# Products ahead of a norm: the first weight tiles run on the unnormalised residual

## The chip, the cores and the metric

The kernel runs on one core of a Trainium2 chip. The metric is the device time of one execution in microseconds, the median of several runs; the shorter, the better.

## The reference, cut to what matters

The input x is [256 tokens, 1024 features] in float32. The first block adds three mixers, a gated convolutional feed-forward net (FFN) and a gate; then come a pooling layer, an FFN, a dilated attention and another FFN. Each of these reads a root-mean-square norm of the residual, and the ones of the second part are modulated: each feature gets a scale and a shift computed from a condition vector c.

```
def _rmsnorm(x, g):
    x32 = x.astype(jnp.float32)
    y = x32 * lax.rsqrt(jnp.mean(x32 * x32, axis=-1, keepdims=True) + EPS)
    return (y * g.astype(jnp.float32)).astype(x.dtype)

def _modulate(h, shift, scale):
    return h * (1 + scale[:, None, :]) + shift[:, None, :]

h = h + rms_norm(mix, post_mix_norm[i])
f = conv_ffn(rms_norm(h, pre_ffn_norm[i]), w_up[i], conv_w[i], conv_b[i], w_down[i])

def _conv_ffn(h, w_up, conv_w, conv_b, w_down):
    a, v = jnp.split(h @ w_up, 2, axis=-1)
    a = _causal_dwconv(a, conv_w, conv_b)
    return (jax.nn.silu(a) * v) @ w_down
```

The factor of a token (the rsqrt) multiplies a whole row of the norm's output, so a product with a weight matrix may take it before or after.

## The kernel before, in words

Activations lie with features on the 128 partitions: x is `xT`, 8 tiles of 128 features x 256 tokens. Every product is computed to nearly float32 by splitting both sides in a high and a low part: `wr`, `wl` of a weight tile (ScalarE L208 or L211, VectorE L209 or L212) and `R`, `L` of an activation tile. `mm3` (L222 to L224) issues R wr, L wr and R wl; an output tile of 128 features over 1024 inputs is one weight tile and 24 such matmuls of 128x256. Weight tiles come in order from the SP queue; TensorE's sums lie in six buffers `acc`.

A norm goes so: while the last product before it is made, each x tile is squared on ScalarE (`sq`), GpSimd adds the squares up (L251), and TensorE sums them over the partitions (`st <- ones, sq`, L239). `rstd` turns the sums into token factors: VectorE `rv` (L263), GpSimd `rr` (L265), and TensorE spreads them over the partitions (`st <- cst, rr`). `norm_split` then makes, for each of 8 tiles, `ny` = x g rb on VectorE (L288), R on ScalarE (L275 or, with a shift, L278) and L on VectorE (L276, L279); the next products start when the first R and L are there.

Four places matter:
- first norm: `post` (L1077 to L1090) norms the mixer's output F, adds it to x tile by tile (VectorE: F <- F, st at L1088, xT <- xT, F at L1090) and sums the squares of x; then `norm_split` and the products of w_up, the first FFN;
- second: behind `ple_gate`; then pool_w_in and the pooling chain on VectorE (`ps`, L1200 to L1203);
- third: behind pool_w_out (`addg`, L1110); then ffn_w_up0;
- fourth: behind attn_w_o (`addg`); then ffn_w_up1, the last FFN.

The norm ahead of the attention is not touched. The modulation vectors are computed along the way: `ada_rows` (L994 to L1006) loads a weight row group `adw` in four transfers and runs 32 small matmuls on it (`acc <- adw, ccol`), a ScalarE copy `row` and a transpose (`acc <- cst, row`), placed at norms; `ada` does single columns on VectorE (L1051). `ple_vec` norms a side input p (`acc <- pT, raw`).

The order on each engine is set by a scheduler that goes by priority: `norm_split` and `rstd` are marked as high priority, and in `post` the order on VectorE is the program's (`manual_schedule`). `wload` keeps later weight splits behind the last split of a norm (`keep_free`).

Of the kernel before, what the change touches and what calls it, by code (L numbers as in the profile page):

```python
# [9 lines left out]
F32 = mybir.dt.float32  # L10
F32R = mybir.dt.float32r
# [6 lines left out]
T = 256  # L18
D = 1024
KB = 8  # L20
# [6 lines left out]
# modulation columns per weight tile: mixer output, FFN up (every other tile), FFN down, pool, layer 0 up and down,  # L27
# attention, gate
# [15 lines left out]
ORDER = "uswrcSn"  # L44
RATE = ((0,1),(3,2),(2,2),(1,1))

# [27 lines left out]
def _consts():  # L74
    """shape-only constants: masks, identities, distance tables"""
# [15 lines left out]
    d = 128 + p - s                                                   # query 128 + p, key s  # L91
# [40 lines left out]
class Net:  # L132
# [28 lines left out]
    def c(self, name):  # L161
        o, n = COFF[name]
        return self.cst[:, o:o + n]
# [9 lines left out]
    # ------------------------------------------------------------------ setup  # L173
    def setup(self):
# [3 lines left out]
        self.cst = self.const([128, NCST], "cst")  # L178
        nc.sync.dma_start(self.cst[:, 0:128], a["cst"][:, 0:128])
# [5 lines left out]
        self.ident, self.bones, self.cen = self.c("ident"), self.c("bones"), self.c("cen")  # L185
        self.mAR = self.c("mAR").rearrange("p (a t) -> p a t", a=2)
        self.mD, self.mOT, self.blk, self.hsel, self.idc = (self.c(n) for n in ("mD", "mOT", "blk", "hsel", "idc"))
# [6 lines left out]
        self.L = self.const([128, KB, T], "L", F32R)  # L194

    # ------------------------------------------------------- weight streaming
    def wload(self, W, m, k0, kn, width=128):
        """W: DRAM [mt, 128, kb*width]; returns hi and lo parts as [128, kn, width]."""
# [59 lines left out]
    def rstd(self, st, r=None):  # L258
        """token sums of squares [128, 2] -> PSUM [128, T] with rsqrt(mean + eps) on every partition"""
# [11 lines left out]
    def split(self, y, R, L, bias=None):  # L271
        """R + L = y (+ bias), both parts exact in float32r"""
# [18 lines left out]

    def keep_free(self, hold):
# [18 lines left out]
    def mixers(self, rb):  # L311
        tc, a = self.tc, self.a
        with tc.tile_pool(name="mx", bufs=1) as mx, tc.tile_pool(name="mxp", bufs=2, space=PSUM) as self.px:
            self.mx = self.tp = mx
            self.rbs = self.mxt([128, T], "rbs")
# [20 lines left out]
    def mix_rw(self):  # L336
# [7 lines left out]
        # feature tiles of w_in: 0-2 r, 3-5 k, 6-8 v, 9 decay|aaa, 10 gate, 11-13 q, 14 kc, 15 vc,  # L344
        # 16 ks, 17 kw, 18-19 s5
        for m in (9, 10, 3, 4, 5, 0, 1, 2, 6, 7, 8):
            pz = self.psum("acc", self.nacc)
            self.lin(W, m, pz[:, 0:T], self.R, self.L, chunk=4 if m == 9 else KB)
            if m == 10:
                nc.sync.dma_start(self.cst[:, 128:NCST], a["cst"][:, 128:NCST])  # L350
# [73 lines left out]
    def rwkv(self):  # L424
# [32 lines left out]
        # cumulated log decays per chunk of 64 tokens  # L457
# [1035 lines left out]
```

## Time and profile before

| | |
|---|---|
| median of 3 runs | 1277.03 us (1273.57 to 1280.05) |
| profiled execution, first to last instruction (span) | 1274.8 us |
| its mean granted TensorE clock | 0.954 |
| busy: TensorE, VectorE, ScalarE, GpSimd | 94%, 72%, 53%, 9% |

The profile gives no time of the profiled execution beside its span, so the span stands for it. In a row, PE is TensorE (PEld its weight loads), DVE VectorE, ACT ScalarE, POOL GpSimd; `out<-in` are the program's tile names, and a number in brackets is the time for which the engine was idle before, with what ended it. A granted clock of 1.00 is 2.4 GHz and of 0.50 is 1.2 GHz.

### The profile page before, as it was taken

To read this page: it belongs to the slowest core of one execution; us is meant where nothing else is said; L and a number is where in the kernel's file an instruction comes from. 1 tells how busy PE (TensorE), PEld (TensorE's weight loads), DVE (VectorE), ACT (ScalarE), POOL (GpSimd) and SP (SyncE) were. 2 spreads that over 40 slices of the span, in tenths; PEclk is the share of its full clock that TensorE was granted. 3 is DMA by queue.
4 is the path that set the end of the run, shared out by engine and by line. 5 is a ranking of instruction groups with operands and counts; after the bars stand their busy time and mean duration, and the time that the engine had idled before them with its cause. 6 is when DMAs were issued, how large, how long until landed. Compare 5 with 4: busy or idle time off the path is not lost. (4 is left out here: it accounts for less than half of the span.)

```text
span 1274.8 us, 26289 instructions
## 1 busy us (share of the span) xinstructions
PE 1199.6 (94%) x10644; PEld 1133.5 (89%) x10644; DVE 919.7 (72%) x1771; ACT 669.9 (53%) x1159; POOL 114.0 (9%) x139
## 2 busy tenths in 40 slices
PE   5998898899999988889999997999999998999996
PEld 5976676899999987879999997999999988999996
DVE  6899855489999657868898866756665756777753
ACT  7633643466665544545565436545555554655541
POOL 0027300220000102020000010000000002000010
PEclk9998988899999988888999998999999998999998
DMA  7522300566677875476887874665555523555661
GB/s 279 169 73 72 134 18 10 182 232 247 232 243 268 314 243 194 164 270 219 284 299 256 311 280 161 230 219 199 181 201 176 203 84 117 198 193 204 199 182 33
DMA packets 71834, 247.71 MB, mean 194 GB/s; under 512 B 8224, under 2 KB 10528, under 8 KB 71712
## 3 DMA queue, kind: packets, MB, share of 16 engines
q1 hardware_dynamic: 71424, 245.24, 55.7%
q8 instruction: 83, 1.36, 0.4%
q10 hardware_dynamic: 288, 0.79, 0.2%
q14 instruction: 39, 0.32, 0.1%
HBM read 244.95 MB, written 1.05 MB: 193 GB/s over the span
## 5 line engine op out<-in xcount | busy, mean ns | idle before, releaser
L222 PE MATMUL acc<-R,wr 128*128 128x256 f32 x1792 | 507.6, 285 | 6.3 <-ACT wr L211 3.8
L224 PE MATMUL acc<-R,wl 128*128 128x256 f32 x1792 | 508.6, 284 | 2.8 <-DVE wl L212 1.8
L223 PE MATMUL acc<-L,wr 128*128 128x256 f32 x1792 | 507.7, 284 | 3.4 <-DVE L L279 3.4
L209 DVE TENSOR_TENSOR wl<-raw,wr 128x1024 fp32r<-128x1024 f32 (+2 forms) x298 | 351.3, 1183 | 132.9 <-ACT wr L208 132.2
L208 ACT CAST wr<-raw 128x1024 fp32r<-128x1024 f32 (+2 forms) x298 | 301.5, 1015 | 253.1 <-PE acc L223 208.0
L222 PEld LDWEIGHTS acc<-R,wr 128*128 128x128 f32 x1792 | 344.5, 193 | 12.4 <-ACT wr L211 4.1
L223 PEld LDWEIGHTS acc<-L,wr 128*128 128x128 f32 x1792 | 346.0, 193 | 6.1 <-DVE L L279 3.8
L224 PEld LDWEIGHTS acc<-R,wl 128*128 128x128 f32 x1792 | 344.4, 192 | 7.1 <-DVE wl L212 2.9
L222 PE MATMUL acc<-aR,wr 128*128 128x256 f32 x608 | 169.5, 282 | 4.8 <-ACT aR L275 4.7
L223 PE MATMUL acc<-aL,wr 128*128 128x256 f32 x608 | 169.9, 281 | 1.0 <-DVE aL L276 1.0
L224 PE MATMUL acc<-aR,wl 128*128 128x256 f32 x608 | 169.5, 281 | 1.3 <-DVE wl L209 1.2
L251 POOL TENSOR_TENSOR sq<-sq,sq 128x256 f32<-128x256 f32 x48 | 56.1, 1169 | 910.1 <-ACT sq L247 896.7
L1051 DVE SCALAR_TENSOR_TENSOR adw<-adw,cond 128x1024 f32<-128x1024 f32 x84 | 103.5, 1234 | 39.9 <-DMA adw<-in_ada_dram 39.5
L222 PEld LDWEIGHTS acc<-aR,wr 128*128 128x128 f32 x608 | 114.8, 190 | 5.4 <-ACT aR L275 5.1
L224 PEld LDWEIGHTS acc<-aR,wl 128*128 128x128 f32 x608 | 114.8, 189 | 1.9 <-DVE wl L209 1.9
L223 PEld LDWEIGHTS acc<-aL,wr 128*128 128x128 f32 x608 | 115.1, 189 | 1.3 <-DVE aL L276 1.2
L212 DVE TENSOR_TENSOR wl<-raw,wr 128x1024 fp32r<-128x1024 f32 (+3 forms) x50 | 60.6, 1211 | 26.8 <-ACT wr L211 26.8
L211 ACT CAST wr<-raw 128x1024 fp32r<-128x1024 f32 (+3 forms) x50 | 50.7, 1014 | 53.8 <-PE acc L223 41.3
L1121 DVE SCALAR_TENSOR_TENSOR fy<-acc,vec,fy 128x254 f32<-128x254 f32 (+1 forms) x132 | 62.9, 476 | 0.1
L239 PE MATMUL acc<-wr,R 128*128 128x256 f32 x192 | 54.8, 286 | 0.0
L239 PE MATMUL acc<-wr,L 128*128 128x256 f32 x192 | 53.9, 281 | 0.0
L239 PE MATMUL acc<-wl,R 128*128 128x256 f32 x192 | 53.7, 281 | 0.0
(385 smaller groups left out, 1541.8 us busy)
## 6 DMA issues: line engine op xcount, KB each, us to landing
raw<-in_ffn_w_up_dram SPq DMA_DIRECT2D x88, 512.0 KB, 3.6
adw<-in_ada_dram SPq DMA_DIRECT2D x84, 512.0 KB, 5.4
raw<-in_w_up_dram SPq DMA_DIRECT2D x44, 512.0 KB, 3.6
raw<-in_ffn_w_down_dram SPq DMA_DIRECT2D x32, 512.0 KB, 4.3
adw<-in_ada_r_dram SPq DMA_DIRECT2D x28, 512.0 KB, 5.9
raw<-in_attn_w_q_dram SPq DMA_DIRECT2D x24, 512.0 KB, 6.7
raw<-in_w_k_dram SPq DMA_DIRECT2D x24, 512.0 KB, 3.7
raw<-in_w_v_dram SPq DMA_DIRECT2D x24, 512.0 KB, 3.8
```

The lines of the kernel that those rows point to most:

```text
L208: nc.scalar.copy(wr, raw)
L209: nc.vector.tensor_sub(wl, raw, wr[:].bitcast(F32))
L211: nc.scalar.copy(wr, raw)
L212: nc.vector.tensor_sub(wl, raw, wr[:].bitcast(F32))
L222: mm(out, wr, xr, start=start, stop=False)
L223: mm(out, wr, xl, start=False, stop=False)
L224: self.last_mm = mm(out, wl, xr, start=False, stop=stop).ins
L239: self.nc.tensor.matmul(out, lhsT, rhs, start=start, stop=stop)
L251: nc.gpsimd.tensor_tensor(sq, sq, self.sqsum, op=ALU.add)
L1051: nc.vector.scalar_tensor_tensor(w, w, 1.0, self.cond, op0=ALU.mult, op1=ALU.mult, accum_out=self.mod[:, i:i + 1])
L1121: nc.vector.scalar_tensor_tensor(out[:, sh:T], pz[:, 0:T - sh], cw(tap), out[:, sh:T], op0=ALU.mult, op1=ALU.add)
```

## The change

At the four norms, as soon as an x tile is there, `x g` (g the norm's weights, with the modulation's scale) is split in two parts `raw_x` (R on ScalarE, L on VectorE). The first four weight tiles of the next matrix (two pairs for an FFN) run on these, 96 matmuls, and their results are multiplied by the token factors, kept in `rbq`, when they leave `acc`. Where there is a modulation shift, it rides along as two further columns (128x258 instead of 128x256), and is added after the factor. The other weight tiles run on the normed R and L as before. At the first norm the parts of `x g` are R and L themselves and the normed parts lie in `raw_x`. The constants of the mixers move to the mixers' pool.

```
+    def ahead_split(self, k):
+        nc, g = self.nc, self.rawg[:, k:k + 1]
...
+        with self.tc.high_priority():
+            nc.scalar.activation(v(R), x, AF.Identity, scale=g)
+            nc.vector.scalar_tensor_tensor(v(L), x, g, v(R.bitcast(F32)), op0=ALU.mult, op1=ALU.subtract)
+
+    def ahead_lin(self, W, m, ps):
+        n = self.rawn
+        self.lin(W, m, ps[:, 0:n], self.rawR[:, :, 0:n], self.rawL[:, :, 0:n])
+        return ps
...
     def post(self, W, R, L, g, kb, hook=None, stat=False):
...
                 if stat and k < KB:
                     nc.vector.tensor_tensor(self.xT[:, k], self.xT[:, k], F[:, k], op=ALU.add)
+                    nc.scalar.activation(self.rawR[:, k, 0:T], self.xT[:, k], AF.Identity, scale=self.rawg[:, k:k + 1])
+                    nc.vector.scalar_tensor_tensor(self.rawL[:, k, 0:T], self.xT[:, k], self.rawg[:, k:k + 1],
+                                                   self.rawR[:, k, 0:T].bitcast(F32), op0=ALU.mult, op1=ALU.subtract)
                     self.sq_stat(st, self.xT[:, k], k, pre=False)
...
-    def addg(self, W, R, L, g, kb, hook=None, perm=False):
+    def addg(self, W, R, L, g, kb, hook=None, perm=False, ahead=False):
...
             self.nc.vector.scalar_tensor_tensor(x, z, g[:, m:m + 1], x, op0=ALU.mult, op1=ALU.add)
+            if ahead:
+                self.ahead_split(m)
...
+    def up_ahead(self, W, n):
+        ps = []
+        for m in range(n):
+            ps.append([self.ahead_lin(W, i, self.psum("acc", self.nacc)) for i in (m, FT + m)])
+        return ps
...
+            if m < len(ps):
+                z = [self.tmp([128, 2 + T], "fz", bufs=4) for _ in range(2)]
+                for i in range(2):
+                    nc.vector.tensor_tensor(z[i][:, 2:], ps[m][i][:, 0:T], self.rbq, op=ALU.mult)
...
     def second(self, st):
         nc, a = self.nc, self.a
+        ps = [self.ahead_lin(a["pool_w_in"], m, self.psum("acc", self.nacc)) for m in range(AHEAD[0])]
         rb = self.rstd(st[:, 0:2])
-        g = self.scaled_gain("ga0", self.modv(8), self.vcol("norm1_g_2", 0, 8))
-        self.norm_split(self.xT, rb, g, self.R, self.L, self.modv(0))
-        st = self.pool_mixer(lambda m: self.ada(ADA[3]))
+        self.keep_r(rb)
+        self.norm_split(self.xT, rb, self.ga0, self.R, self.L, self.modv(0))
+        st, g = self.pool_mixer(lambda m: self.ada(ADA[3]), ps)
         self.dump("x3", self.xT)
+        ps = self.up_ahead(a["ffn_w_up0"], AHEAD[1])
         self.ada_rows(ROWS[3])
         rb = self.rstd(st[:, 0:2])
-        g = self.scaled_gain("gb0", self.modv(32), self.vcol("norm2_g_2", 0, 8))
+        self.keep_r(rb)
         self.norm_split(self.xT, rb, g, self.R, self.L, self.modv(24))
```

Three places in the order of the engines' instructions. VectorE, first norm, the loop in `post` that forms x; before:

```order
L263 TENSOR_SCALAR rv_2786<-st_2503 128x2
L1088 TENSOR_TENSOR F_2502<-F_2502,st_2790 128x256
L1090 TENSOR_TENSOR xT<-xT,F_2502 128x256
L1088 TENSOR_TENSOR F_2502<-F_2502,st_2790 128x256
L1090 TENSOR_TENSOR xT<-xT,F_2502 128x256
```

and now:

```order
L263 TENSOR_SCALAR rv_2788<-st_2505 128x2
L1124 TENSOR_TENSOR F_2504<-F_2504,st_2792 128x256
L1126 TENSOR_TENSOR xT<-xT,F_2504 128x256
L1128 SCALAR_TENSOR_TENSOR L<-xT,vec,R 128x256
L1124 TENSOR_TENSOR F_2504<-F_2504,st_2792 128x256
L1126 TENSOR_TENSOR xT<-xT,F_2504 128x256
L1128 SCALAR_TENSOR_TENSOR L<-xT,vec,R 128x256
```

Each tile has a third instruction, the low part L of x g, which reads the R that ScalarE makes from the x tile of the row above it.

TensorE, second norm, from the modulation rows to the first products; before:

```order
L239 MATMUL acc_5886<-adw_5907,ccol 32x128 x8
L239 MATMUL st_5579<-ones_81,sq_5842 128x1 x2
L239 MATMUL st_5579<-ones_81,sq_5882 128x1 x2
L239 MATMUL acc_5886<-adw_5917,ccol 32x128 x4
L239 MATMUL st_5980<-cst,rr_5978 128x128 x2
L239 MATMUL acc_5886<-adw_5917,ccol 32x128 x4
L239 MATMUL acc_5931<-adw_5932,ccol 32x128 x8
L239 MATMUL acc_5886<-cst,row_5927 128x4
L222 MATMUL acc_6019<-R,wr_6022 128x256
L222 MATMUL acc_6059<-R,wr_6062 128x256
```

and now:

```order
L239 MATMUL acc_5939<-adw_5960,ccol 32x128 x8
L239 MATMUL st_5616<-ones_81,sq_5893 128x1 x2
L239 MATMUL acc_5939<-adw_5970,ccol 32x128 x8
L239 MATMUL st_5616<-ones_81,sq_5935 128x1 x2
L239 MATMUL acc_5939<-cst,row_5980 128x4
L239 MATMUL acc_5984<-adw_5985,ccol 32x128 x8
L222 MATMUL acc_6029<-raw_x,wr_6032 128x258
L223 MATMUL acc_6029<-raw_x,wr_6032 128x258
```

After these stand 17 more products with raw_x, and only then `st <- cst, rr`, which spreads the token factors: the new products, the transpose of `row` and eight matmuls of the next row group have moved ahead of it.

VectorE, third norm, from the first `ny` on; before:

```order
L288 SCALAR_TENSOR_TENSOR ny_6840<-xT,gb_6834,st_6831 128x256
L288 SCALAR_TENSOR_TENSOR ny_6844<-xT,gb_6834,st_6831 128x256
L288 SCALAR_TENSOR_TENSOR ny_6848<-xT,gb_6834,st_6831 128x256
L1051 SCALAR_TENSOR_TENSOR adw_6836,mod<-adw_6836,cond 128x1024
L279 SCALAR_TENSOR_TENSOR L<-ny_6840,mod,R 128x256
L279 SCALAR_TENSOR_TENSOR L<-ny_6844,mod,R 128x256
```

and now:

```order
L288 SCALAR_TENSOR_TENSOR ny_7047<-xT,gb_6563,st_7043 128x256
L288 SCALAR_TENSOR_TENSOR ny_7051<-xT,gb_6563,st_7043 128x256
L288 SCALAR_TENSOR_TENSOR ny_7055<-xT,gb_6563,st_7043 128x256
L1194 TENSOR_TENSOR fz_7084<-acc_6870,rbq 128x256
L1194 TENSOR_TENSOR fz_7085<-acc_6901,rbq 128x256
L1194 TENSOR_TENSOR fz_7105<-acc_6932,rbq 128x256
L212 TENSOR_TENSOR wl_7204<-raw_7201,wr_7203 128x1024
L279 SCALAR_TENSOR_TENSOR L<-ny_7047,mod,R 128x256
```

The evictions `fz`, which need the sums of the products with raw_x, and a weight split stand between the norm's `ny` and its low parts L; the modulation column (`adw`, `mod`) that stood there comes later.

## Rows read from the trace of the kernel before

**Rows 1.** Page: busy time; VectorE's weight splits; modulation rows' transfers (us to landing).

```profile
PE 1199.6 (94%) x10644; PEld 1133.5 (89%) x10644; DVE 919.7 (72%) x1771; ACT 669.9 (53%) x1159; POOL 114.0 (9%) x139
...
L209 DVE TENSOR_TENSOR wl<-raw,wr 128x1024 fp32r<-128x1024 f32 (+2 forms) x298 | 351.3, 1183 | 132.9 <-ACT wr L208 132.2
...
adw<-in_ada_r_dram SPq DMA_DIRECT2D x28, 512.0 KB, 5.9
```

**Rows 2.** Waits of TensorE: total us, times, longest us.

```profile
PE acc L239 <- DMA adw<-in_ada_r_dram: 9.3, 4, 3.0
```

**Rows 3.** Windows: us, busy PE PEld DVE ACT POOL, granted clock, DMA share, GB/s.

```profile
275.00:300.00 25.00, 25.00 (x215) 25.00 (x214) 23.70 (x44) 15.90 (x25) 0.00 (x0) 1.00 0.67 232
511.00:545.00 34.00, 28.97 (x224) 28.30 (x224) 28.58 (x66) 20.07 (x46) 0.67 (x6) 0.90 0.54 188
579.10:582.10 3.00, 3.00 (x16) 3.00 (x15) 2.79 (x8) 1.52 (x3) 0.00 (x0) 0.50 0.00 0
1100.00:1150.00 50.00, 50.00 (x444) 50.00 (x443) 35.79 (x56) 29.30 (x47) 0.00 (x0) 1.00 0.59 196
```

**Rows 4.** Timeline, TensorE, first norm: start us, us, [idle before <- releaser].

```profile
256.60 1.22 PE L239 MATMUL st<-cst,rr 128*128 128x128 f32 x4
...
258.74 6.78 PE L239 MATMUL acc<-pT,raw 128*128 128x256 f32 x28
...
266.80 0.47 PE L222 MATMUL acc<-R,wr 128*128 128x256 f32 x1
...
275.43 0.36 PE L222 MATMUL acc<-R,wr 128*128 128x256 f32 x1
```

**Rows 5.** Timeline, VectorE, first norm.

```profile
245.63 0.42 DVE L1088 TENSOR_TENSOR F<-F,st 128x256 f32<-128x256 f32 x1 [1.59 <-PE st L239]
246.08 0.43 DVE L1090 TENSOR_TENSOR xT<-xT,F 128x256 f32<-128x256 f32 x1
246.43 0.41 DVE L1088 TENSOR_TENSOR F<-F,st 128x256 f32<-128x256 f32 x1
```

**Rows 6.** Lines 305 and 306: ns min/median/max.

```profile
L305 ACT ACTIVATE R<-xT,vec x8: 492/498/511, 9.2 to 12.2; 128x256 fp32r<-128x256 f32 x8
...
L306 DVE SCALAR_TENSOR_TENSOR L<-xT,vec,R x8: 476/478/485, 9.7 to 12.9; 128x256 fp32r<-128x256 f32 x8
```

**Rows 7.** Timeline, TensorE, second norm and pooling.

```profile
493.27 1.05 PE L239 MATMUL st<-ones,sq 128*128 128x1 f32 x8 [1.03 <-POOL sq L251]
497.23 0.65 PE L239 MATMUL acc<-adw,ccol 128*32 128x128 f32 x8 [2.90 <-DMA adw<-in_ada_r_dram]
497.81 1.22 PE L239 MATMUL st<-cst,rr 128*128 128x128 f32 x4
...
500.85 0.99 PE L222 MATMUL acc<-R,wr 128*128 128x256 f32 x3
...
535.16 1.01 PE L222 MATMUL acc<-aR,wr 128*128 128x256 f32 x3 [4.19 <-ACT aR L275]
```

**Rows 8.** Timeline, VectorE, second norm.

```profile
499.07 1.26 DVE L288 SCALAR_TENSOR_TENSOR ny<-xT,ga,st 128x256 f32<-128x256 f32 x3 [4.48 <-PE st L239]
```

**Rows 9.** Timeline, TensorE, third norm.

```profile
562.59 0.86 PE L239 MATMUL acc<-adw,ccol 128*32 128x128 f32 x24
...
569.46 0.80 PE L222 MATMUL acc<-R,wr 128*128 128x256 f32 x2
...
572.12 0.58 PE L223 MATMUL acc<-L,wr 128*128 128x256 f32 x1 [1.62 <-DVE L L279]
...
585.17 0.28 PE L224 MATMUL acc<-R,wl 128*128 128x256 f32 x1
```

**Rows 10.** Timeline, TensorE, fourth norm.

```profile
1072.55 0.28 PE L224 MATMUL acc<-oR,wl 128*128 128x256 f32 x1
...
1077.97 0.58 PE L222 MATMUL acc<-R,wr 128*128 128x256 f32 x1 [1.11 <-ACT R L278]
...
1093.38 0.28 PE L224 MATMUL acc<-R,wl 128*128 128x256 f32 x1
```

More of the change, by code (lines that the diff above doesn't have):

```diff
@@ L44 @@
 ORDER = "uswrcSn"
+AHEAD = (4, 2)
 RATE = ((0,1),(3,2),(2,2),(1,1))
@@ L290, in norm_split, with ahead, keep_r @@
         self.keep_free(hold)
+    def ahead(self, tile, gain, bias=None, order=lambda t: t):
+        nc = self.nc
+        self.rawg, self.raw, self.raw_order = gain, tile, order
+        self.rawR, self.rawL = tile[:, :, 0], tile[:, :, 1]
+        self.rawn = T + 2 if bias is not None else T
+        if bias is not None:
+            b = bias.unsqueeze(2).to_broadcast([128, KB, 2])
+            nc.scalar.copy(tile[:, :, 0, T:T + 2], b)
+            nc.vector.tensor_sub(tile[:, :, 1, T:T + 2], b, tile[:, :, 0, T:T + 2].bitcast(F32))
+    def ahead_split(self, k):
+        nc, g = self.nc, self.rawg[:, k:k + 1]
+        v = lambda t: t.rearrange("p (c a) -> p c a", c=2) if self.raw_order(self.xT[:, k]).ndim == 3 else t
+        R, L, x = self.rawR[:, k, 0:T], self.rawL[:, k, 0:T], self.raw_order(self.xT[:, k])
+        with self.tc.high_priority():
[5 more added lines that the diff above has]
+        return ps
+    def keep_r(self, rb, order=lambda t: t):
+        o = order(rb)
+        q = self.rbq[:].rearrange("p (c a) -> p c a", c=2) if o.ndim == 3 else self.rbq
+        with self.tc.high_priority():
+            self.nc.scalar.copy(q, o)
     def keep_free(self, hold):
@@ L1133, in ffn_up @@
             y = self.tmp([128, T], "fy", bufs=2)
-            self.conv(pz[:, 0:T], col(m), bias(m), y)
             v = self.tmp([128, T], "fv", bufs=2)
+            if m < len(ps):
+                z = [self.tmp([128, 2 + T], "fz", bufs=4) for _ in range(2)]
+                for i in range(2):
+                    nc.vector.tensor_tensor(z[i][:, 2:], ps[m][i][:, 0:T], self.rbq, op=ALU.mult)
+                if shift:
+                    nc.scalar.activation(z[0][:, 0:2], ps[m][0][:, T:T + 2], AF.Copy, scale=-1.0)
+                    b = self.tmp([128, 2], "fb", bufs=2)
+                    nc.scalar.copy(b[:, 0:1], ps[m][1][:, T:T + 1])
+                    nc.vector.scalar_tensor_tensor(b[:, 1:2], ps[m][0][:, T:T + 1], cws[:, m:m + 1], bias(m), op0=ALU.mult,
+                                                   op1=ALU.add)
+                    nc.scalar.activation(y, z[0][:, 2:], AF.Identity, scale=col(m)(2), bias=b[:, 1:2])
+                    for tap in (1, 0):
+                        nc.vector.scalar_tensor_tensor(y, z[0][:, tap:tap + T], col(m)(tap), y, op0=ALU.mult, op1=ALU.add)
+                    nc.scalar.activation(y, y, AF.Silu)
+                    nc.vector.scalar_tensor_tensor(v, z[1][:, 2:], b[:, 0:1], y, op0=ALU.add, op1=ALU.mult)
+                    self.split(v, self.aR[:, m], self.aL[:, m])
+                    if hook:
+                        hook(m)
+                    continue
+                pa, pb = z[0][:, 2:], z[1][:, 2:]
+            else:
+                pz = self.psum("acc", self.nacc)
+                self.lin(W, m, pz[:, 0:T], R, L)
+                self.lin(W, FT + m, pz[:, T:2 * T], R, L)
+                pa, pb = pz[:, 0:T], pz[:, T:2 * T]
+            self.conv(pa, col(m), bias(m), y)
             if conv_both:
                 nc.scalar.activation(y, y, AF.Gelu_apprx_tanh)
-                self.conv(pz[:, T:2 * T], col(FT + m), bias(FT + m), v)
+                self.conv(pb, col(FT + m), bias(FT + m), v)
                 nc.vector.tensor_tensor(v, v, y, op=ALU.mult)
@@ L1238, in attention_layer @@
             self.ap_ = self.tp = ap
-            self.R2 = ap.tile([128, KB, T], F32R, name="R2")
-            self.L2 = ap.tile([128, KB, T], F32R, name="L2")
+            self.R2, self.L2 = (self.rawt[:, :, i, 0:T] for i in range(2))
             self.norm_split(self.xT, rb, g, self.R, self.L, self.modv(48), self.by_parity)
```

83 lines of the change are left out of this document (56 added, 27 removed).

## The prediction

> **What bounds the kernel now.** I read four views: the page's busy times, the waits of the matmul engine, then the timelines of the four norms that the change touches, then the busy times by stretch. The page shows TensorE busy for 94% of the span [rows 1]: the products are the kernel, and what is left to win is the time in which it waits or runs at the lower of its two clocks. The longest of its waits at these norms are for the transfers of the modulation rows, 9.3 us at four places [rows 2]. Behind the norms it also runs slow: a stretch of 3.00 us at granted clock 0.50 (1.2 GHz) shows 16 records, two of them at its edges, 0.21 us for a product [rows 3]; at clock 1.00 (2.4 GHz) it is 0.116 us (25.00/215) in the first FFN and 0.113 us (50.00/444) in the last [rows 3]. Each low stretch follows one in which the engine waited or did small work. VectorE stands close behind: 23.70 us of 25.00 in the first FFN, 28.58 of 34.00 in the pooling, but only 35.79 of 50.00 in the last FFN [rows 3].
>
> **The change, norm by norm.** At each norm 96 products (four weight tiles) no longer need the norm. For it eight pairs of splits are added where x forms, and 4 evictions take the token factor. Nearest rows: the same operation ahead of the first product takes 0.498 us on ScalarE and 0.478 on VectorE [rows 6], and VectorE starts such instructions some 0.39 us apart (three in 1.26 [rows 8]). The evictions multiply by the factors as F does, 0.45 us from one start to the next [rows 5]. Per norm VectorE gets 8 x 0.39 + 4 x 0.45 = 4.9 us more. Below I follow what ends last.
>
> **First norm.** Here the order puts all 96 products behind the second statistic, so they cover nothing of it. But the loop that forms x gets longer: VectorE's queue has F, x, L for each tile, and L waits for ScalarE's R of the same tile, behind which the next F stands. Before, a tile takes 246.43 - 245.63 = 0.80 us, 0.45 for F and 0.35 for x [rows 5]. Now x must end (0.43), ScalarE starts (0.09, estimate), R takes 0.50, a hop of 0.05 (estimate), and L's 0.39: with F's 0.45 that is 1.91. Eight tiles: 15.3 instead of 6.4 us, 9 us more. The second statistic's token factors stand before at 256.60 + 1.22 = 257.8 [rows 4], partly behind modulation rows that now go later, so that 5.8 of the 9 stay: 263.6. From there some 20 products at 0.21 and 76 at 0.116 end at 276.6, then the modulation rows and the products of the side input (1.5 and 2.7 at the full clock), a transfer that is issued behind them and awaited (median of its kind 5.9 [rows 1], part of it covered), and the kernel stands at some 284.7 with 96 products done. Before: products begin at 266.80, 61 have begun by 275.43 [rows 4], and 284.7 comes with 61 + 9.27/0.116 = 141. The difference of 45 x 0.116 is **5 us lost**. Bounds: if the side work fits between products as before, only the 5.8 less the earlier begin of the products, some 1 lost; if VectorE's evictions and the transfer add up, 9 lost.
>
> A rule of the Trainium skill (TensorE: Matmul & The Clock Gate, Engine queue depths) speaks here: ScalarE and VectorE take their queues strictly in order, so the waiting L holds up the next F. No row of before has a waiting split with other work behind it in that loop. By the rule the term is the 5 us above; without it the loop would be 8 x (0.45 + 0.35 + 0.39) = 9.5 us, and the term nothing, which is the first rival.
>
> **Second norm.** The token factors are due some 495.4 (the last square sum 493.27 + 1.05, then VectorE and GpSimd, some 1.1), but run at 497.81, because TensorE stands at a modulation product for a transfer, 2.90 us until 497.23 [rows 7]. The change leaves that wait where it is, and puts more behind it: the row's transpose, which waits for a ScalarE copy, eight products of the next row, and 18 of the new products. From 497.23: 0.65 + 0.5 + 1.0 + 1.1 = 500.5, then 18 products at mixed clock to 503.3, so the factors are ready at 504.0 to 504.5. The norm's own split on VectorE starts there instead of at 499.07 [rows 8]; behind it VectorE has its pooling chain, for which TensorE waits 4.19 us until 535.16 [rows 7]. Half of the 5 us is made good, since weight splits and the first pooling steps now precede or overlap the split. I take **2 us lost**; bounds 6 lost (nothing made good) and 3 gained (the first four pooling tiles need no split now; if that brings them early enough, most of the wait of 4.19 goes).
>
> **Third norm.** Last product before 562.59; then sums, factors and rows, two products at 569.46, the third at 572.12 for VectorE's L, and by 585.17 only 58 have begun, most at the lower clock [rows 9]. Now the engine goes on with 28, 10, 28 and 30 new products between the sums, at full clock, and has 96 done some 12.5 us after the last product (96 x 0.113 and 1.6 for sums and factors). The factors come at 8.5 to 9, the normal split's L stand behind evictions and weight splits, and the last L ends at some 23.4. At 24.1 the engine has begun 96 + 48 (the pairs of tiles that had their k in time), before it had 58 + 13 = 71. 73 x 0.113 = **8 us gained**. Bounds: 3, if the modulation columns' work slides between the L's as it does now; 11, if it never stops.
>
> **Fourth norm** (ahead of the last FFN). First products before at 1077.97, then at the lower clock, 117 by 1093.38 [rows 10]. Now 96 are done 12.9 us (96 x 0.113 and 2 for sums and factors) after the last product (1072.8 [rows 10]), the last L comes at 19.9, and at 20.6 there are 144: 27 x 0.113 = **3 us gained**; bounds 1 and 6.
>
> **Small terms.** 288 products are two columns wider: 288 x 2/256 x 0.113 = 0.25 us. The raw splits of norms two to four stand where VectorE has room in the products ahead of the norm (a weight split of 1.18 us [rows 1], one or two operations of 0.4 and the new 0.39, at most 2.4 us a tile against 24 x 0.113 = 2.7 of products), so I cost them at nothing; without that cover it would be 24 x 0.39 = 9 us. No DMA is added or taken away. The constants move to another pool: no instruction more.
>
> **Sum.** -8 - 3 + 5 + 2 + 0.3 = -3.7 us. The profiled execution spans 1274.8 us and lies 2.2 under the median of the runs, 1277.03; 1271.1 + 2.2 gives **1273 us**. 0.5% is 6.4 us, about what a measurement of this kernel can tell from no change.
>
> **Rivals.**
> First: the two early norms cost nothing, because the loop's L does not hold up the next tile or the longer wait is covered. For: before, the first products start only 9 us after the factors [rows 4], so there is slack to eat. Against: the order has L between x and the next F. Then 11 gained less 0.3: 1266 us.
>
> Second, the slower side: VectorE pays its added work in full. Place: the stage behind each norm, where evictions and the remaining split share VectorE with weight splits that TensorE needs. Price: 4 x 4.9 = 20 us against the 11 gained, so 9 lost: 1286. It decides where the stage leaves VectorE less than 4.9 us. For: 1.30 us of 25 free in the first FFN, 5.4 of 34 in the pooling; against: 14 of 50 in the last FFN [rows 3].
> The Trainium skill (VectorE: DVE Perf Modes, the TRN2 errata) has every instruction pay a fixed part, so tiles under 512 elements are dear: its 58 + 256 cycles at 0.96 GHz give an estimate of 0.33 us, 48 x 0.33 = 16 us for the price above, and 1282 instead of 1286. The spacing of 0.39 in the rows is longer and decides.
>
> Third: the change does all it can, no wait and no low clock at the last three norms. From the counts above: third 585.17 - 562.59 - 58 x 0.113 - 5 of small work = 11; fourth 20.6 - 117 x 0.113 - 2 = 5; second, 10 between 490.7 and 500.85 less 3 of small work, and nothing lost at the first: 23 in all, 1254. Against: the second norm's rows still wait for their transfer.
>
> **How the numbers follow.** Forecast 0.48 (own range 1267 to 1279), first rival 0.22, second 0.20, third 0.06, others 0.04. The ends of the bounds, added as if independent, are about 6 us to each side of 1273, and with the rivals the range that leaves out under 2 in 10 is 1260 to 1286. Faster by over 0.5% is under 1270.6: 0.22 of the forecast, most of the first rival, all of the third: 0.36. Slower is over 1283.4: a little of the forecast and two thirds of the second: 0.18. The rest is 0.46.
>
> **What would show it.** First norm: x forming every 1.9 us, factors at some 21 us after the last product of the mixer's output instead of 15. Second: TensorE still waits for a modulation row's transfer ahead of the factors, and VectorE's norm split starts 4 to 6 us later. Third and fourth: granted clock near 1.0 behind the last product, no stop for L in the first 20 us. It would be wrong if the loop keeps 0.8 us a tile, if the factors of the second norm no longer wait, or if TensorE waits for L or for an eviction between the 96 products and the next.

## The result, and the profile after

| | before | after |
|---|---|---|
| median of 6 runs each, on one chip | 1275.76 us (1271.01 to 1282.02) | 1285.96 us (1279.71 to 1290.34) |
| span of the profiled execution | 1274.8 us | 1288.5 us |

The changed kernel is slower: ratio 1.0071, 95% interval 1.0045 to 1.0097, some 9 us where 4 us of gain were forecast. The forecast of 1273 had the wrong sign; 1286 is the last microsecond of its range.

The busy line of the page after, to hold against [rows 1]:

```profile
PE 1202.7 (93%) x10644; PEld 1136.9 (88%) x10644; DVE 942.8 (73%) x1830; ACT 686.2 (53%) x1210; POOL 113.0 (9%) x139
```

TensorE has as many instructions as before and 3 us more busy time, so most of the 13.7 us between the two profiled spans is time in which TensorE stands still. To find where they lie I cut every execution at VectorE's instructions `rv` (L263), which follow the last square sum of a norm: they are in all kernels, and between two of them stands one stage. Stage A goes from the first changed norm through its FFN, B from there through the gate, the second norm and the pooling, C through the third norm and its FFN, D through attention, the fourth norm and the last FFN.

| us | start | A | B | C | D |
|---|---|---|---|---|---|
| before | 243.9 | 214.0 | 107.5 | 200.1 | 498.5 |
| before, another execution | 238.6 | 215.2 | 105.4 | 201.4 | 497.8 |
| after | 243.2 | 224.5 | 115.0 | 191.5 | 503.1 |
| after, another execution | 241.5 | 224.3 | 114.1 | 191.0 | 497.1 |

The start holds the same instructions in all kernels and still varies by almost 8 us from one execution to the next (238.6 to 246.3), so a span by itself says little here. Between two executions of one kernel the stages differ by some 2 us at most, but for D of after. Over all the kernels below that leave a stage's code alone, A lies between 214.0 and 217.5, B between 105.0 and 107.5, C between 197.7 and 202.6 and D between 497.8 and 504.4. A and B lose and C gains by more than that; D's 503.1 is mostly a chance of one execution (below, on the hardware).

**First norm.** TensorE's timeline after, against [rows 4] (x1 to x48 is the number of instructions in a row, the bracket the idle time before and its releaser):

```profile
246.79 1.01 PE L239 MATMUL acc<-ones,sq 128*128 128x1 f32 x4 [1.82 <-ACT sq L247]
248.64 1.01 PE L239 MATMUL acc<-ones,sq 128*128 128x1 f32 x4 [0.84 <-ACT sq L247]
...
262.71 1.22 PE L239 MATMUL st<-cst,rr 128*128 128x128 f32 x4 [1.95 <-POOL rr L265]
...
277.69 5.45 PE L239 MATMUL acc<-pT,raw 128*128 128x256 f32 x24
...
285.29 0.47 PE L222 MATMUL acc<-raw_x,wr 128*128 128x256 f32 x1
```

The square sums of two tiles begin 248.64 - 246.79 = 1.85 us apart. VectorE's queue shows why, against [rows 5]:

```profile
245.01 0.42 DVE L1124 TENSOR_TENSOR F<-F,st 128x256 f32<-128x256 f32 x1 [1.59 <-PE st L239]
245.46 0.42 DVE L1126 TENSOR_TENSOR xT<-xT,F 128x256 f32<-128x256 f32 x1
246.46 0.49 DVE L1128 SCALAR_TENSOR_TENSOR L<-xT,vec,R 128x256 fp32r<-128x256 f32 x1 [0.57 <-ACT R L1127]
246.87 0.41 DVE L1124 TENSOR_TENSOR F<-F,st 128x256 f32<-128x256 f32 x1
```

VectorE stands idle for 0.57 us in front of L until ScalarE's R is there, and the next tile's F starts behind it. The factors stand at 262.71 + 1.22 = 263.9, and the 96 products done ahead are followed by the rows and the side input until 285.29.

**Second norm.** TensorE after, against [rows 7]; the last product of the gate ends just ahead of the first row:

```profile
500.50 1.52 PE L239 MATMUL acc<-adw,ccol 128*32 128x128 f32 x48
506.49 1.01 PE L239 MATMUL st<-ones,sq 128*128 128x1 f32 x4 [4.47 <-POOL sq L251]
...
508.65 1.02 PE L239 MATMUL st<-ones,sq 128*128 128x1 f32 x4
...
511.03 0.58 PE L222 MATMUL acc<-raw_x,wr 128*128 128x258 f32 x1
...
515.07 1.06 PE L239 MATMUL st<-cst,rr 128*128 128x128 f32 x4
```

The wait for a row's transfer, 2.90 us in [rows 7], is gone; in its place TensorE waits 4.47 us for the square sums, and the spread of the factors begins 14.6 us behind the gate's products (before, 497.81 - 490.7 = 7.1). VectorE in the same stretch:

```profile
498.96 0.96 DVE L1259 TENSOR_TENSOR xT<-xT,fy 128x256 f32<-128x256 f32 x1
...
501.02 1.75 DVE L209 TENSOR_TENSOR wl<-raw,wr 128x1024 fp32r<-128x1024 f32 x1
502.70 0.94 DVE L311 SCALAR_TENSOR_TENSOR raw_x<-xT,ga,raw_x 128x256 fp32r<-128x256 f32 x1
...
504.64 1.22 DVE L209 TENSOR_TENSOR wl<-raw,wr 128x1024 fp32r<-128x1024 f32 x1
505.77 0.94 DVE L1258 TENSOR_TENSOR fy<-fy,E 128x256 f32<-128x256 f32 x1
...
507.04 0.41 DVE L1259 TENSOR_TENSOR xT<-xT,fy 128x256 f32<-128x256 f32 x1
```

The last x is formed at 507.04, 6.5 us after the gate's last product, behind two weight splits and three raw splits, of which one is shown; and the same small operation takes 0.41 us or 0.96.

**Third norm.** TensorE after, against [rows 9]:

```profile
590.09 1.52 PE L239 MATMUL acc<-adw,ccol 128*32 128x128 f32 x48
...
594.83 0.64 PE L239 MATMUL acc<-adw,ccol 128*32 128x128 f32 x16 [0.96 <-DMA adw<-in_ada_r_dram]
...
600.10 0.38 PE L223 MATMUL acc<-L,wr 128*128 128x256 f32 x1 [1.30 <-DVE L L279]
...
601.64 0.58 PE L223 MATMUL acc<-L,wr 128*128 128x256 f32 x1 [0.57 <-DVE L L279]
```

The last product of the pooling begins at 577.05, and the new ones follow it without a stop. The stops for L are still there, at the 39th and 45th product with the norm, the 135th and 141st in all, where before the third one stopped.

**Fourth norm**, against [rows 10], two of its four such stops (0.53, 0.22, 0.61 and 0.26):

```profile
1099.82 0.38 PE L223 MATMUL acc<-L,wr 128*128 128x256 f32 x1 [0.53 <-DVE L L279]
...
1103.38 0.38 PE L223 MATMUL acc<-L,wr 128*128 128x256 f32 x1 [0.61 <-DVE L L279]
```

### The profile page after: what moved, and what is told of

The parts are those of the page before. It is cut to its first block, busy times and chain, and to the rows that moved or that the text cites. A ratio compares the mean times of both kernels' runs of the same rounds, so it can differ in the third digit from the quotient of the medians.

```text
span 1288.5 us, 26402 instructions
## 1 busy us (share of the span) xinstructions
PE 1202.7 (93%) x10644; PEld 1136.9 (88%) x10644; DVE 942.8 (73%) x1830; ACT 686.2 (53%) x1210; POOL 113.0 (9%) x139
## 4 chain that ended last, share of the span: by engine, by line
PE 66%; DVE 5%; DMA 4%; ACT 2%; issue 2%; POOL 1%; POOLq 0%; SPq 0%; ACTq 0%; DVEq 0%
PE acc L222 18%; PE acc L223 18%; PE acc L224 18%; PE acc L239 6%; PE sx L239 2%; PE po L239 2%; DMA adw<-in_ada_r_dram 2%; DVE wl L209 2%; PE tx L1430 1%; DMA adw<-in_ada_dram 1%; DMA raw<-in_ffn_w_down_dram 1%; PE st L239 1%; POOL sq L251 1%; DVE adw L1087 0%; ACT wr L208 0%
## 5 line engine op out<-in xcount | busy, mean ns | idle before, releaser
L222 PE MATMUL acc<-R,wr 128*128 128x256 f32 x1184 | 335.7, 286 | 4.3 <-ACT wr L211 3.3
L223 PE MATMUL acc<-L,wr 128*128 128x256 f32 x1184 | 335.8, 284 | 3.7 <-DVE L L279 3.2
L224 PE MATMUL acc<-R,wl 128*128 128x256 f32 x1184 | 335.8, 284 | 1.9 <-DVE wl L212 1.7
L222 PEld LDWEIGHTS acc<-R,wr 128*128 128x128 f32 x1184 | 227.4, 193 | 10.0 <-ACT wr L211 3.6
L223 PEld LDWEIGHTS acc<-L,wr 128*128 128x128 f32 x1184 | 229.6, 194 | 6.2 <-DVE L L279 4.5
L224 PEld LDWEIGHTS acc<-R,wl 128*128 128x128 f32 x1184 | 227.8, 193 | 4.2 <-DVE wl L212 2.5
L223 PE MATMUL acc<-raw_x,wr 128*128 128x256 f32 (+1 forms) x608 | 173.7, 286 | 0.0
L224 PE MATMUL acc<-raw_x,wl 128*128 128x256 f32 (+1 forms) x608 | 172.5, 284 | 0.8 <-DVE wl L209 0.8
L222 PE MATMUL acc<-raw_x,wr 128*128 128x256 f32 (+1 forms) x608 | 172.2, 284 | 0.6 <-ACT wr L208 0.6
L1087 DVE SCALAR_TENSOR_TENSOR adw<-adw,cond 128x1024 f32<-128x1024 f32 x84 | 104.0, 1240 | 33.2 <-DMA adw<-in_ada_dram 32.7
L224 PEld LDWEIGHTS acc<-raw_x,wl 128*128 128x128 f32 x608 | 115.7, 190 | 2.3 <-issue 1.4
L222 PEld LDWEIGHTS acc<-raw_x,wr 128*128 128x128 f32 x608 | 116.0, 191 | 1.5 <-ACT wr L208 0.8
L223 PEld LDWEIGHTS acc<-aL,wr 128*128 128x128 f32 x608 | 115.0, 189 | 2.1 <-DVE aL L276 2.1
L223 PEld LDWEIGHTS acc<-raw_x,wr 128*128 128x128 f32 x608 | 115.3, 190 | 0.5 <-issue 0.5
```

The lines of the kernel that those rows point to most:

```text
L222: mm(out, wr, xr, start=start, stop=False)
L223: mm(out, wr, xl, start=False, stop=False)
L224: self.last_mm = mm(out, wl, xr, start=False, stop=stop).ins
L1087: nc.vector.scalar_tensor_tensor(w, w, 1.0, self.cond, op0=ALU.mult, op1=ALU.mult, accum_out=self.mod[:, i:i + 1])
```

## Experiments

All but the last two were timed beside the kernel before on their own chip. A line number above 200 is 7 or more lines further in these kernels than in the changed one. The edits are cut to what they do; in the kernels, switches choose between the old and the new code.

**One norm at a time.** Four kernels keep the changed code at one norm and the old code at the others.

```diff
+ON = (1, 0, 0, 0)        # and (0,1,0,0), (0,0,1,0), (0,0,0,1)
-            self.ahead_split(m)
+            if ON[1]:
+                self.ahead_split(m)
-        ps = self.up_ahead(a["ffn_w_up0"], AHEAD[1])
+        ps = self.up_ahead(a["ffn_w_up0"], AHEAD[1]) if ON[2] else ()
...
```

> The change at the first norm alone. Theory (by the trace of after): the longer loop on VectorE and the side work that now stands behind the 96 products cost 9 to 10 us, more than the 5 forecast: 1285 against 1276, ratio 1.007. Rival: what is seen there comes from the other norms' use of the shared tile raw_x or of VectorE; then alone it costs the 5 us forecast, ratio 1.004.

> The change at the second norm alone. Theory: VectorE cannot take the eight low parts and one more weight split beside the gate's work, so the square sums come some 5 us later behind the last product, and TensorE, which has the wait for the modulation row there anyway, loses 5 us in all: ratio 1.004. Rival (forecast): nothing is lost ahead of the norm, 2 us behind it: ratio 1.0015.

> The change at the third norm alone. Both theories expect a gain: by the trace of after 5.6 us (ratio 0.9956), by the forecast 8 us (0.9937). If the gain there is only time shifted from an earlier stage, it is 0.

> The change at the fourth norm alone. In the traces 960 products of the last FFN stand 113.3 ns apart before and 117.8 after, both at granted clock 1.00, 4.3 us in all. Theory 1: this spacing comes from the way the engine enters the stage, without the stretch at the lower clock, so it is caused by the change here: no gain or up to 3 us lost, and 117.8 again. Theory 2: the spacing falls out by chance in each execution: then it is 113.3 or 117.8 here whatever the change, and the time on average 1.6 us better (ratio 0.9987). Forecast: 3 us gained, ratio 0.9976.

| norm | ratio to before, 95% interval | its stages by the trace |
|---|---|---|
| first | 1.0123 (1.0081 to 1.0164) | A 228.4 |
| second | 1.0071 (1.0042 to 1.0101) | B 112.3 |
| third | 1.0004 (0.9979 to 1.0030) | B 108.8, C 194.0 |
| fourth | 1.0005 (0.9984 to 1.0027) | D 498.7 |

The two early norms carry the whole loss, and neither late one is a loss. Three of the four came out otherwise than expected: the first and the second lose more than either text says, and the third shows no gain in its time, where both expected 5 to 8 us. The last FFN of the fourth stands at 113.3 ns, which speaks against the first theory there.

In the executions without the stage's change, A is 215.7 on average (11 of them), B 106.2, C 200.3 and D 499.2 (D without one of 504.4, whose last FFN has the slower spacing described below). Against these the trace gives +8.7 for the first norm in the two executions of after. The 228.4 of the first norm alone is 12.7 above; a part of that is a wait of 2.05 us for a weight tile of the down products, which is 0.85 in after and 0.48 in before. The second norm comes to +5.8 to +6.1 and the third to -5.1 (C -7.7, and B +2.6: `rv` comes 5.7 us behind the pooling's last product, before 3.0). The fourth comes to -1.5, again without the execution of after that has the slower spacing; that is less than D itself varies by.

The medians do not add up as the stages do: 15.5 + 8.0 + 0.5 + 0.3 = 24 us, and after has 10.

**First norm: the wait in the loop.** The norm alone, with L of tile k - 1 issued behind F and x of tile k.

```diff
                     nc.vector.tensor_tensor(self.xT[:, k], self.xT[:, k], F[:, k], op=ALU.add)
                     nc.scalar.activation(self.rawR[:, k, 0:T], self.xT[:, k], AF.Identity, scale=...)
-                    nc.vector.scalar_tensor_tensor(self.rawL[:, k, 0:T], ...)
                     self.sq_stat(st, self.xT[:, k], k, pre=False)
+                if stat and k:
+                    self.raw_low(k - 1)
```

> The first norm alone, with VectorE's low part of a tile put behind the next tile's F and x (the wait for ScalarE's R is then covered). Theory (the loop's wait is the larger part of the loss): a tile takes 0.45 + 0.35 + 0.39 = 1.2 us instead of 1.85, the second statistic comes 5 us earlier than in e1, and 5 us of its loss go: ratio to before 1.006 to 1.008 where e1 had 1.012. Rival (the loss is the side work that stands behind the 96 products, not the loop): the loop is shorter but the time stays within 2 us of e1.

1.0034 (1.0012 to 1.0055), A 218.4. VectorE's queue in this kernel:

```profile
241.52 0.41 DVE L1132 TENSOR_TENSOR F<-F,st 128x256 f32<-128x256 f32 x1
241.97 0.42 DVE L1134 TENSOR_TENSOR xT<-xT,F 128x256 f32<-128x256 f32 x1
242.31 0.48 DVE L1152 SCALAR_TENSOR_TENSOR L<-xT,vec,R 128x256 fp32r<-128x256 f32 x1
242.71 0.41 DVE L1132 TENSOR_TENSOR F<-F,st 128x256 f32<-128x256 f32 x1
```

No idle time in front of L, 242.71 - 241.52 = 1.19 us a tile and not 1.85, with the same instructions. The stage from the first `rv` to the second falls from 17.5 to 12.5 us (10.2 without the change), and A by 6 of the 8.7. The wait behind which the next tile queues is the larger part of this norm's loss.

**First norm: the side work.** As above, and the modulation rows and the side input's norm are emitted ahead of the 96 products instead of behind them.

```diff
-        ps = n.up_ahead(a["w_up"], AHEAD[1])
         n.keep_r(rb)
         n.ada_setup()
         n.ada_rows(ROWS[0])
...
         n.ple_vec()
+        ps = n.up_ahead(a["w_up"], AHEAD[1])
```

> As e5, and the side work (modulation rows and the side input's products) ahead of the 96 products, as it stood before the change. Theory: the loss shrinks to the loop's three added parts, 8 x 0.39 = 3 us: ratio 1.002 to 1.004. If the side work's place costs nothing, it is as e5.

1.0005 (0.9984 to 1.0027), A 217.4. With both moves the norm costs nothing that these runs can tell from none, and gains nothing. Both kernels come out a little better than their theories.

**Second norm: two suspects.** The norm alone, once without the eight raw low parts (zeros are read in their place) and once with the modulation rows behind the factors instead of ahead of them.

```diff
# without the low parts
-            nc.vector.scalar_tensor_tensor(v(L), x, g, v(R.bitcast(F32)), op0=ALU.mult, op1=ALU.subtract)
# rows late
-            n.ada_rows(ROWS[2])
             rb = n.second(st)
...
         rb = self.rstd(st[:, 0:2])
         self.keep_r(rb)
+        self.ada_rows(ROWS[2])
         self.norm_split(self.xT, rb, self.ga0, self.R, self.L, self.modv(0))
```

> The second norm alone, without the eight low parts of x g on VectorE (their tile is set to zero once, and the products read that, so the result is not the reference's). Theory (VectorE's backlog delays the last x tiles and square sums): the last square sum comes again 2.5 to 3.5 us behind the last product instead of 8.1 in after, and most of the loss of e2 (9 us by the runs, 5.6 by the profile) goes: ratio 1.000 to 1.003. Rival (TensorE's order, factors behind 18 products and two rows, is what costs): the square sums come earlier but the time stays at e2's 1.005 to 1.007.

> The second norm alone, with the modulation rows behind the token factors instead of ahead of them: the 96 products then stand directly behind the last product of the gate. Theory (VectorE's backlog): TensorE is busy through the norm, but the factors still wait for VectorE, so a third to a half of the loss goes: ratio 1.003 to 1.005. Rival (TensorE's order): the loss goes entirely or turns into a gain of up to 5 us: ratio 0.996 to 1.000.

Without the low parts 1.0062 (1.0033 to 1.0090), B 112.2; rows late 1.0034 (1.0006 to 1.0061), B 108.9. Neither frees the norm alone. TensorE without the low parts:

```profile
492.65 1.52 PE L246 MATMUL acc<-adw,ccol 128*32 128x128 f32 x48
498.00 1.00 PE L246 MATMUL st<-ones,sq 128*128 128x1 f32 x4 [3.84 <-POOL sq L258]
...
502.81 1.20 PE L246 MATMUL st<-cst,rr 128*128 128x128 f32 x4
503.94 1.08 PE L246 MATMUL acc<-adw,ccol 128*32 128x128 f32 x14
```

The square sums still come late (3.84 us of idle time against 4.47), so the theory fails here: the last x is done 6.2 us after the gate's last product begins, where it is 8.3 with the low parts and 2.1 in the kernel before. The low parts are a third of that delay. Two weight splits still stand in front of the last x, and no run took those away.

**Both together:**

> The second norm alone, with the modulation rows behind the factors (as e8) and without VectorE's eight low parts (as e7; the products read zeros for them, so the result is not the reference's). Theory (two causes, each hiding the other): from the gate's end to the end of the pooling the loss, 6.1 us in e2, 5.9 in e7, 2.7 in e8, is 0 to 1 here. Rival (TensorE's order alone): 2.7 as e8.

1.0012 (0.9990 to 1.0035), B 105.9. The loss is gone. TensorE:

```profile
490.76 0.28 PE L229 MATMUL acc<-raw_x,wr 128*128 128x258 f32 x1
...
496.36 0.50 PE L246 MATMUL st<-ones,sq 128*128 128x1 f32 x4
...
501.79 0.61 PE L246 MATMUL st<-cst,rr 128*128 128x128 f32 x4
```

The products with raw_x now start 0.12 us behind the gate's last one (490.64) and run through to the factors.

B also holds the gate's own products, and the gate lasts 30.4 to 32.7 us in all kernels but the one of the next experiment, whichever their change: the shorter where the granted clock in it is 0.94 or 0.95, the longer where it is 0.89 or 0.90. So the stage is better cut at the gate's last product:

| us | the gate | its last product begins | from there to the third norm's `rv` |
|---|---|---|---|
| before | 32.6 | 490.51 | 74.8 |
| second norm alone | 32.7 | 492.50 | 79.6 |
| without the low parts | 32.3 | 492.44 | 79.9 |
| rows late | 30.4 | 485.21 | 78.5 |
| both | 30.7 | 490.64 | 75.2 |

The six executions with neither the second nor the third norm's change have 74.0 to 75.3, on average 74.7. So the loss of 4.9 us is 5.2 without the low parts, 3.8 with the rows late and 0.5 with both (the 6.1, 5.9 and 2.7 of the expectation are differences of B). There are two causes, and each hides most of the other's removal. Every figure is of one execution; by the times of the runs the rows late give half of the loss back alone (1.0034 where 1.0071 stood), so how much each hides is less sure than that both together take the loss away.

The time of the factors is not what decides. Their spread begins 10.4 us behind the beginning of the gate's last product without the low parts and 11.1 with both moves. But in the first kernel TensorE makes no product until then, only rows and sums, and the granted clock falls; in the second it makes products all the way. The windows of both, with the columns of [rows 3]:

```profile
492.80:504.80 12.00, 7.39 (x94) 5.64 (x86) 6.62 (x12) 4.74 (x12) 2.38 (x4) 0.72 0.76 275
```

```profile
490.80:501.80 11.00, 10.93 (x91) 10.60 (x90) 8.54 (x11) 7.27 (x15) 2.61 (x4) 1.00 0.49 172
```

By which way the low parts still cost some 3 us once the rows are late is not shown.

**Second norm: GpSimd.** Rows late, and the squares are summed on TensorE tile by tile, so that GpSimd adds none.

```diff
-            self.sq_stat(st, self.xT[:, m], m)
+            self.sq_stat(st, self.xT[:, m], m, pre=False)
```

> As e8 (rows behind the factors, low parts kept), and the squares of the gate's x tiles summed on TensorE tile by tile instead of added up on GpSimd first. Theory: the square sums no longer wait for GpSimd's 1 us a tile, and VectorE's adds, which take 0.95 us instead of 0.42 where GpSimd works at the same time, are shorter; so the loss of 2.7 us in e8 goes to 0 to 1. Rival (VectorE's added instructions themselves): 2 to 3 as e8.

1.0072 (1.0043 to 1.0102), B 108.5: no gain over rows late (1.0034, 108.9) by either. VectorE in this kernel:

```profile
495.69 0.42 DVE L1273 TENSOR_TENSOR fy<-fy,E 128x256 f32<-128x256 f32 x1
496.02 0.48 DVE L319 SCALAR_TENSOR_TENSOR raw_x<-xT,ga,raw_x 128x256 fp32r<-128x256 f32 x1
```

Every such operation takes 0.41 to 0.49 us here and none takes 0.94. This does not acquit GpSimd, though. From the gate's last product on the stage lasts 73.2 us, 5.2 less than with the rows late alone and less than without the change. What is gained there is lost in the gate, which lasts 35.3 us: 20 matmuls of the square sums now stand between its products, these come 117.2 ns apart where rows late has 113.8 (before has 117.2 too), and the granted clock in it is 0.90 instead of 0.94. So whether the contention is a part of this norm's loss stays open. The whole time is longer, by 1.0072, than the stages explain; that stays open too.

**What the late norms give.** Norms three and four together, and then with three pairs of weight tiles ahead instead of two, with six buffers for the evictions.

```diff
-AHEAD = (4, 2)
+AHEAD = (4, 3)
-                z = [self.tmp([128, 2 + T], "fz", bufs=4) for _ in range(2)]
+                z = [self.tmp([128, 2 + T], "fz", bufs=6) for _ in range(2)]
```

> The change at the third and fourth norm alone. Theory: these two are the ones that do not lose: 6 us gained at the third by the traces, 0 to 2 at the fourth: ratio 0.994 to 0.997. Rival (e3 and e4, by their medians): no gain, ratio 0.999 to 1.001.

> As e11, with three pairs of weight tiles ahead of the norm instead of two (144 products). In after the 96 products at the third norm were done 12.9 us behind the last product, and the normed parts came until 24. Theory: the engine then no longer stops for the low parts L: another 2 to 4 us gained on the third norm, ratio 0.991 to 0.995. Rival: the additional evictions stand ahead of the L's in VectorE's queue and push them back as far: same as e11.

Two pairs: 0.9983 (0.9957 to 1.0009), median 1272.98. Three pairs: 0.9931 (0.9908 to 0.9954), median 1267.07 against 1275.60: faster than both kernels. Its third norm:

```profile
581.89 1.52 PE L246 MATMUL acc<-adw,ccol 128*32 128x128 f32 x48
...
587.18 0.64 PE L246 MATMUL acc<-adw,ccol 128*32 128x128 f32 x16
...
589.58 0.38 PE L230 MATMUL acc<-L,wr 128*128 128x256 f32 x1 [0.87 <-DVE L L286]
```

C is 187.6, 12.7 less than without the change (9.8 with B's +2.9 taken off). The wait for a row's transfer (0.9 us with two pairs) is gone, and one stop for L of 0.87 is left, where the kernel with two pairs has one of 2.77: the 48 further products cover most of what the L's came too late. At the fourth norm no stop is left.

**The two kernels again**, one execution each, to see what repeats.

> The kernel before, unchanged, profiled a second time. Theory (the spacing of the products at granted clock 1.00 falls out anew at each rise of the clock, in each execution): some stage that stood at 113.3 ns now stands near 117.8 or the other way round, with the same instructions. Rival (it belongs to the program: its addresses and its order): every FFN has the spacing it had, 117.8, 113.3 and 113.3 ns.

> The changed kernel, unchanged, profiled a second time. Theory (by chance): the last FFN may stand at 113.3 ns as in e1 to e4, and the span is then 4 us shorter than the first profile's 1288.5. Rival (it belongs to the program): 117.8 ns again. By both the first norm loses 9 to 10 us and the second 5.

1271.1 and 1281.57 us; their stages stand in the first table. A, B and C repeat within 2.1 us; D of after does not (497.1 against 503.1). The two answers differ: in the kernel before every FFN has the spacing it had, as the rival said, and in the changed kernel the last FFN went from 117.8 to 113.3 ns, as the theory said.

## Why the prediction was wrong

The likeliest of its cases fell, by the sizes of its first three terms above all. By the trace the terms came out as +8.7, +5.8, -5.1 and -1.5, together +7.9, where +5, +2, -8 and -3 stood. The mechanism at the first norm was right and its price too small; at the second norm a cost that was put at nothing came out as several us; at the third and fourth the stages show the gain, and too much of it was counted.

**First norm, 5 lost forecast, 8.7 measured.** The mechanism was right: L waits for R, the next F behind it, 1.85 us a tile against 1.91, the factors at 263.9 against 263.6, and the first product behind the side work at 285.29 against 284.7. The trace agrees with the rule of the Trainium skill that was weighed there (TensorE: Matmul & The Clock Gate, Engine queue depths), that VectorE takes its queue strictly in order: the same instructions without the waiting L in front take 1.19 us a tile and the stage is 6 us shorter. The mis-sized term is "the kernel stands at some 284.7 with 96 products done. Before: ... 284.7 comes with ... 141": at 285.29 the statistic of the side input was still to come, and the 61 products that before has begun by 275.43 [rows 4] already pay for it. The deficit against the executions without the change is 6.2 us by the 100th product and 8.7 by the 200th, so that is some 2.5 us. With the side work ahead of the 96 products it does not grow there (2.6 and 2.7), with L later alone it does (1.5 and 3.7). About 1 us more comes from the spacing of the products with raw_x (below): 9.5 by the 1200th.

**Second norm, 2 lost forecast, 5.8 measured.** The step that failed is the one in the small terms: "The raw splits of norms two to four stand where VectorE has room in the products ahead of the norm ..., so I cost them at nothing". There was no such room ahead of the last tiles of the gate. Before, `rv` comes 3.7 us behind the gate's last product, after 9.3: VectorE still has raw splits, and weight splits for the products ahead, in front of the last x. The raw splits on VectorE are the smaller part of it: without them `rv` still comes 8.3 us after the gate's last product begins, in the kernel with this norm alone 10.5, in the kernel before 3.9. The forecast took the wait for a row's transfer, 2.90 us [rows 7], to stay the last thing ahead of the factors; instead the square sums came later than the transfer. Both together delayed the factors by 7.5 us (497.81 to 503.3 was forecast, 5.5). Behind them 1.7 of the 7.5 come back by B, some 2.5 by the cut at the gate's last product, and not 3.5; TensorE's wait of 4.19 us in the pooling [rows 7], of which the forecast hoped for some back, has become four waits for the pooling chain's tiles of 6.4 in all (1.37, 1.60, 0.37 and 3.07).

**Third norm, 8 gained forecast, 5.1 measured.** The new products stand between the sums as forecast, 28, 10, 28 and 30, and 24.1 us behind the pooling's last product 140 products have begun, where 144 were forecast and before 71: 69 x 0.113 = 7.8 us up to there. The sum stopped counting at that point. The stop of 0.57 us lies just there, and behind it TensorE runs at the lower clock once more (25 products in the 4 us from 602, at a granted clock of 0.64), so that 5.1 are left of it in B and C together. The 71 was also a low draw: at the same point 60 to 85 products have begun in the 11 executions without this norm's change, 77 on average and 83 in the other one of the same kernel, so the lead was nearer 63 products, 7.1 us.

**Fourth norm, 3 gained forecast, 1.5 measured**, within its bounds of 1 and 6 and within what D varies by. Here the sign "no stop for L in the first 20 us" did not hold: the first of the four small stops begins 15.7 us behind the last product (1083.55).

**The rivals.** The second rival's number, 1286, is what was measured, and its mechanism is half of it: VectorE's added work is paid ahead of the statistic, at the first two norms, and not "in the stage behind each norm" at 4.9 us each. Taking the low parts alone away at the second norm changes nothing (B 112.2 against 112.3), and the late norms gain. That its number is the measured one is luck: it sets 4.9 us lost at each of four norms against 11 gained, and no norm came out so. So it is not shown as it was put. The first rival (the early norms cost nothing) comes true at the first norm once L is put one tile later and the side work early; as changed, it does not.

**Open.** Why the medians of the single-norm kernels add to 24 us and the third's median shows none of the 5 us that its stages show is not settled: the start and the spacing of products move by as much from one execution to the next. Nor is a traced execution a typical one: that of the third norm alone is the fastest of its twelve (1270.64 us, median 1276.03), that without the low parts the slowest of its ten (1291.92, median 1283.67). I did not try a raw_x without its two further columns.

## What to carry to other kernels

Work that is put ahead of a barrier to fill it also lengthens the chain that leads to the barrier; price it there, on the engine that forms the last tile, before the gain behind it is counted. In a queue that goes strictly in order, put an operation that waits for another engine one tile later, with the next tile's work in front of it. Where removing one suspect changes nothing, remove two together before acquitting either.

## What the runs showed of the hardware

**Two spacings at full clock.** With granted clock 1.00, the products of a stage stand either 113.3 or 117.8 ns apart, for the whole stage. The program alone does not fix which: the last FFN of the changed kernel has one in one execution and the other in the other. Nor does it fall out anew everywhere: the kernel before has 117.8, 113.3 and 113.3 ns in its three FFNs both times, and the first FFN in old code has 117.8 in all 11 executions. Windows of five traces follow, with the columns of [rows 3]. The last FFN of after:

```profile
1110.00:1190.00 80.00, 80.00 (x681) 80.00 (x680) 57.09 (x89) 45.49 (x72) 0.00 (x0) 1.00 0.60 198
```

The same FFN of the same kernel in its other execution:

```profile
1105.00:1180.00 75.00, 75.00 (x664) 75.00 (x663) 55.50 (x87) 44.59 (x71) 0.00 (x0) 1.00 0.61 203
```

80/681 is 117.5 ns and 75/664 is 113.0. The slower one comes without the change too, as in the kernel with the second norm alone and no low parts, whose last FFN is the old code (117.5, where [rows 3] have 112.6):

```profile
1110.00:1190.00 80.00, 80.00 (x681) 80.00 (x681) 55.11 (x86) 45.32 (x71) 0.00 (x0) 1.00 0.55 186
```

The FFN behind the third norm, in old code, in the kernel with the fourth norm alone:

```profile
590.00:670.00 80.00, 80.00 (x682) 80.00 (x681) 72.87 (x133) 47.33 (x73) 0.00 (x0) 1.00 0.84 293
```

And in the kernel before:

```profile
590.00:670.00 80.00, 80.00 (x708) 80.00 (x708) 73.25 (x133) 47.85 (x75) 0.00 (x0) 1.00 0.85 292
```

Over some 960 products that is 4 us, as much as a term of the forecast, and most of D's 503.1 against 497.1. DMA share and the other engines' load are alike in the last pair, so neither explains it; the cause is open.

**Products with raw_x** come 118.9 ns apart in the first FFN of all five executions that have the first norm's change, and 117.8 in the 11 others. The window of after:

```profile
300.00:380.00 80.00, 80.00 (x675) 80.00 (x675) 73.05 (x133) 50.93 (x85) 0.00 (x0) 1.00 0.65 229
```

And the same window of before:

```profile
300.00:380.00 80.00, 80.00 (x682) 80.00 (x681) 74.17 (x135) 52.13 (x86) 0.00 (x0) 1.00 0.67 236
```

These products are 256 columns wide like the old ones; what differs is the tile that they read, whose rows are 258 long and hold R and L in turn. The two were not tried apart.

**VectorE beside GpSimd.** The VectorE operations that took 0.94 and 0.96 us above lie beside these of GpSimd:

```profile
498.56 1.08 POOL L251 TENSOR_TENSOR sq<-sq,sq 128x256 f32<-128x256 f32 x1 [1.61 <-ACT sq L247]
...
502.10 1.26 POOL L251 TENSOR_TENSOR sq<-sq,sq 128x256 f32<-128x256 f32 x1 [0.41 <-ACT sq L247]
505.71 0.73 POOL L251 TENSOR_TENSOR sq<-sq,sq 128x256 f32<-128x256 f32 x1 [2.34 <-ACT sq L247]
```

VectorE's operation from 505.77 ends at 506.71, 0.27 us after GpSimd's ends at 506.44; the one from 502.70 ends at 503.64, 0.28 after 503.36. It waits until GpSimd is done. The Trainium skill states this (SBUF — State Buffer, SBUF: two separate sides: an operation of VectorE with two inputs in SBUF and one of GpSimd share a pair of ports, and the one that comes second waits until the first is done); the trace agrees, with 0.94 us against 0.41 to 0.48, and with 0.41 to 0.49 throughout where GpSimd adds nothing.
